# Every other pair of the stick-breaking mixer transposed in 32-blocks on VectorE, and a handicap for VectorE in the choice of engines

## The chip, the core and the metric

The kernel runs on one core of one Trainium2 chip. The metric is the device time of one execution in microseconds. Before the change the median of three runs is 1145.74 us (1144.85 to 1147.17). A separate execution was recorded by the hardware profiler; it took 1142.08 us, 1140.3 us of them between its first and its last instruction.

The engines go by the names of the profile: PE (TensorE), PEld (its weight loads), DVE (VectorE), ACT (ScalarE), POOL (GpSimd), SP (SyncE, which issues most DMAs).

## What is computed

Two layers of a decoder trunk, 512 tokens wide and 1024 features deep, all in float32. Each layer normalises its input, projects it, runs three causal token mixers side by side on the projections and merges them through gates. The mixer that the change is about is the third one, stick-breaking attention with 8 heads of 64:

```python
def hybrid_layer(x, c_silu, ...):
    u = rms_norm(x, norm_g) * (1 + scale) + shift
    z = u @ w_in        # split into aq ak av ag iq ik iw  bq bk bv bg  cq ck cv cg  ma mb mc
    ya = dsa_attention(...)            # A: indexer picks 128 keys per query, softmax attention
    yb = swa_sinks_attention(...)      # B: window of 128 keys, softmax with a sink
    yc = stick_breaking_attention(cq, ck, cv)
    merged = sum(sigmoid(m_b) * ((y_b * silu(gate_b)) @ w_br_b) for b in "abc")
    return x + gate * (merged @ w_out)

def stick_breaking_attention(q, k, v):       # per block of 128 queries
    z = einsum('bthd,bshd->bhts', qb, k) * dh ** -0.5
    log_1m = where(strict, log_sigmoid(-z), 0)
    after = reverse_cumsum(log_1m) - log_1m
    a = where(strict, exp(log_sigmoid(z) + after), 0)
    return einsum('bhts,bshd->bthd', a, v)
```

## The kernel before

All products of a projection run on PE as three passes of 512 columns: each weight chunk of 128 rows is loaded into `wstage`, split into a high part `whi` (a cast) and a low part `wlo` (a subtraction), and multiplied as `whi*uh + whi*ul + wlo*uh`. So PE's work on one chunk of four 128-row blocks is twelve matmuls of 512 columns, and ACT, DVE or POOL do one cast and one subtraction for it.

The mixers work on pairs of heads, four pairs (0 to 3) each, in the order C, B, A. For a pair of the C mixer, `c_qk(p)` (L1191) multiplies queries by keys into five PSUM banks (`ps_s`), in high parts first and then in one uninterrupted group of low parts (`low_parts`, L1179). The value product of the pair before rides in that same group (`RIDE`, L51): pair 0's in `c_qk(1)`, pair 1's in `c_qk(2)`, pair 2's in `c_qk(3)`; pair 3's comes alone afterwards (`GROUPS`). Each bank then goes through a mask, |z|, exp, ln and a reverse scan on DVE (`tensor_tensor_scan`, 511 columns), and a last exp on ACT leaves the weights in a tile `t`, queries in the partitions.

The value product needs keys in the partitions, so the weights of a pair are transposed first, in `softmax_tr`. There are two ways:

- the way of the C mixer before: 20 PE transposes of 128 x 128 (`ps_s<-small,t` in the profile; `small` holds the identity) into five banks, and five copies of 512 columns into the tile `U` on ACT or DVE (`U<-ps_s`);
- the way of the A and B mixers (`TR32`, L47): the normalising step writes the weights in a strided layout into one tile `X` (one buffer for all mixers), four DVE instructions transpose its 32 x 32 blocks in place (`STREAM_TRANSPOSE X<-X`), and sixteen DMAs, issued by SP or ACT as each quarter is ready, move blocks between partition quarters into `U` or, for odd pairs of A and B, into `V5`. In `value_run` (L1404) PE then reads the keys of such a pair in steps.

Nothing runs in the order in which it is written. A `Recorder` collects all instructions with the engines that each may run on, and `forward` (L431) lists them by their latest start, over five rounds (L290), with costs from a table. For an instruction that may run on several engines, `elsewhere` (L558) asks whether another engine would end it earlier; if so, it isn't given to this one. The casts (`cast`: ACT, DVE, and POOL unless the source is in PSUM), the subtractions (`both`: DVE or POOL) and some other steps have such a choice; PE's work has none. DMAs of the 32-block way may be issued by SP or ACT. Each engine then runs its own list strictly in order, so an instruction that waits holds back all behind it on its engine.

In each layer the C mixer runs beside the indexer's selection of keys (`score`, DVE max and match-replace), the gate projections and the queries and keys of the mixers to come. What fills PE between the mixers' steps are the merge gates' projections and the branch products. After the last value product of A comes only such filling and the output projection.

Of the kernel before, what the change touches and what calls it, by code (L numbers as in the profile page):

```python
# [25 lines left out]
F32 = mybir.dt.float32  # L26
F32R = mybir.dt.float32r
BF16 = mybir.dt.bfloat16
AF = mybir.ActivationFunctionType
# [4 lines left out]
P = 128  # L34
# [9 lines left out]
QCOST = 2408  # L44
BKEY = "cfree2"
LOAD_AHEAD, SPLIT_AHEAD = 4, 3
TR32 = {'a': (0, 1, 2, 3), 'b': (0, 1, 2, 3)}  # L47
RIDE = {('c', 1): (0,), ('c', 2): (1,), ('c', 3): (2,), ('a', 1): (0,)}
GROUPS = {'c': ((3,),), 'a': ((1, 2), (3,)), 'b': ((0, 1), (2, 3))}

# [231 lines left out]
class Recorder:  # L282
# [5 lines left out]
    ENTER = {"m": 0.0, "t": 0.035, "c": 0.17, "r": 0.17}  # L288
    TOPORT = 0.13
    ROUNDS = 5  # L290

    def __init__(self, tc, nc, psum, sbuf):
        self.tc, self.nc, self.psum, self.sbuf = tc, nc, psum, sbuf
# [263 lines left out]

    def elsewhere(self, x, name, at, E):  # L558

        end = at + x.alts[name].cost  # L560
        for o, y in x.alts.items():
            if o != name:
                t = max(E[o]["free"], x.est, x.soft.get(o, 0.0), E[o]["port"] if y.port else 0.0) + y.cost
                if t < end - 1e-9:
                    return True
        return False

# [80 lines left out]
def trunk(ctx, tc, xT, vecs, w_ss, w_gt, w_first, w_t, w_v, w_br, w_o, rope, consts, out):  # L648
# [7 lines left out]
    rec = Recorder(tc, nc, ps, sb)  # L656
# [54 lines left out]
    csb, o = small[:, 0:8], 8  # L711
# [63 lines left out]
    st = {}  # L775
# [415 lines left out]
    def c_qk(p):  # L1191
        def fn():
            q = st[f"cq{p}"]
            kh, kl = st[f"ck{p}"]
            zb, pt = [None] * 5, [None] * 5
            for i in (3, 2, 0, 1):
                ts, W = slice(128 * i, 128 * i + 128), 128 * i + 128
                o, first = [None] * 2, [False] * 2
                for e in range(2):
                    bk, c0 = apos(e, i)  # L1200
                    if zb[bk] is None:
                        zb[bk], first[e] = sbank(), True
                    o[e] = zb[bk][:, c0:c0 + W]
                for e in range(2):
                    mm(o[e], q[:, e, ts], kh[:, e, :W], first[e])
                if i == 1:
                    mm(o[1], q[:, 1, ts], kl[:, S:], False)
            low_parts(q, kl, apos, zb, "c", p, LOW_ALL)
            for bk in (0, 3, 1, 4, 2):
                z = zb[bk]  # L1210
                if bk % 3:
                    m = z[:, 256:].rearrange("p (a b) -> p a b", a=2) if bk != 2 else z.rearrange("p (a b) -> p a b", a=2)[:, :, 128:]
                    DVE.tensor_tensor(out=m, in0=m, in1=cmask.unsqueeze(1).to_broadcast([P, 2, P]), op=OP.add)
                else:
                    DVE.tensor_tensor(out=z[:, 384:], in0=z[:, 384:], in1=cmask, op=OP.add)
                t = pt[bk] = t512("t", 10)
                u32 = mybir.dt.uint32
                rec.add({"ACT": ("activation", (t, z, AF.Abs), {}),
                         "DVE": ("tensor_scalar", (t.bitcast(u32), z.bitcast(u32), 0x7FFFFFFF, None), dict(op0=OP.bitwise_and))})
                ACT.activation(t, t, AF.Exp, scale=-1.0)  # L1220
                ACT.activation(t, t, AF.Ln, bias=1.0)
                DVE.scalar_tensor_tensor(t, z, 0.0, t, op0=OP.min, op1=OP.subtract)
                fill(t[:, 511:512], BIG)
                back = t[:, 0:511][:, ::-1]
                DVE.tensor_tensor_scan(back, z[:, 1:512][:, ::-1], back, BIG, op0=OP.add, op1=OP.subtract)
                ACT.activation(t, t, AF.Exp, scale=-1.0)
            st["p", p] = pt
        return op(2700, fn)

    def mixer_c():  # L1230
# [19 lines left out]
    def apos(e, i):  # L1250
        return ((1 + 3 * e, 384), (2, 256 * e), (1 + 3 * e, 0), (3 * e, 0))[i]
# [553 lines left out]
```

## Time and profile before

| | before |
|---|---|
| median of 3 runs | 1145.74 us |
| lowest, highest | 1144.85, 1147.17 us |
| the profiled execution | 1142.08 us |
| its span | 1140.3 us |
| granted clock of PE, mean | 0.996 |
| instructions | 17580 |

The page gives the busy time of each engine, the chain of work that ended last and the groups of instructions. A group's row reads: line, engine, operation, tiles written and read, shape and count, then the busy time of the whole group, the mean duration of one in ns, and the idle time of the engine ahead of them with what ended it. Most instructions have line L620, where the recorder emits them, and those of the uninterrupted low-part and value groups L618; so groups are told apart by their tiles. In the stages, a row gives the busy time of each engine in a stretch of the span, with the number of its instructions.

### The profile page before, as it was taken

To read this page: it belongs to the slowest core of one execution; us is meant where nothing else is said; L and a number is where in the kernel's file an instruction comes from. 1 tells how busy PE (TensorE), PEld (TensorE's weight loads), DVE (VectorE), ACT (ScalarE), POOL (GpSimd) and SP (SyncE) were. 2 spreads that over 40 slices of the span, in tenths; PEclk is the share of its full clock that TensorE was granted. 3 is DMA by queue.
4 is the path that set the end of the run, shared out by engine and by line. 5 is a ranking of instruction groups with operands and counts; after the bars stand their busy time and mean duration, and the time that the engine had idled before them with its cause. 6 is when DMAs were issued, how large, how long until landed. Compare 5 with 4: busy or idle time off the path is not lost.

```text
span 1140.3 us, 17580 instructions
## 1 busy us (share of the span) xinstructions
PE 1123.2 (99%) x5619; PEld 932.7 (82%) x5619; DVE 984.5 (86%) x2238; ACT 530.2 (46%) x1125; POOL 169.4 (15%) x237
## 2 busy tenths in 40 slices
PE   8999999999999999999999999999999999999997
PEld 6899878788887778788898998877888778877886
DVE  7977999999999987888686589999999999777765
ACT  5633767563446442433143247766435455433122
POOL 0100336310013200000000004551101221000001
PEclk9999999999999999999999999999999999999999
DMA  9744332445464573545634442234645455534343
GB/s 351 236 120 122 93 93 84 111 143 152 116 173 148 161 218 121 166 140 177 195 101 108 109 138 78 81 93 121 167 120 139 140 148 147 150 84 142 99 124 107
DMA packets 92764, 157.23 MB, mean 138 GB/s; under 512 B 14080, under 2 KB 28672, under 8 KB 92672
## 3 DMA queue, kind: packets, MB, share of 16 engines
q1 hardware_dynamic: 84608, 143.98, 43.2%
q10 hardware_dynamic: 8064, 12.13, 3.7%
q8 instruction: 44, 0.72, 0.3%
q14 instruction: 48, 0.39, 0.1%
HBM read 125.39 MB, written 4.19 MB: 114 GB/s over the span
## 4 chain that ended last, share of the span: by engine, by line
PE 82%; DVE 11%; DMA 2%; issue 2%; ACT 1%; SPq 0%; POOL 0%; DVEq 0%; ACTq 0%; POOLq 0%
PE ps_z L620 64%; PE ps_s L620 15%; DVE t L620 3%; PE ps_s L618 3%; DVE m L620 1%; DVE score L620 1%; DVE wlo L620 1%; PE ps_z L618 1%; DVE X L620 1%; DMA Y<-in_w_ss 1%; DVE zc L620 1%; DVE Y L620 1%; DVE e L620 0%; SPq L620 0%; DMA V<-X 0%
## 5 line engine op out<-in xcount | busy, mean ns | idle before, releaser
L620 PE MATMUL ps_z<-uh,whi 128*128 128x512 f32 (+1 forms) x905 | 354.1, 393 | 3.7 <-DVE sm L620 2.2
L620 PE MATMUL ps_z<-ul,whi 128*128 128x512 f32 (+1 forms) x905 | 353.1, 391 | 0.3 <-DVE ul L620 0.3
L620 PE MATMUL ps_z<-uh,wlo 128*128 128x512 f32 (+1 forms) x905 | 352.0, 390 | 0.0
L620 DVE TENSOR_TENSOR wlo<-wstage,whi 128x512 fp32r<-128x512 f32 (+2 forms) x322 | 210.8, 657 | 12.4 <-ACT whi L620 4.5
L620 PEld LDWEIGHTS ps_z<-uh,whi 128*128 128x128 f32 x905 | 170.2, 188 | 38.9 <-DVE sm L620 2.6
L620 PEld LDWEIGHTS ps_z<-ul,whi 128*128 128x128 f32 x905 | 170.3, 188 | 34.4 <-issue 1.2
L620 PEld LDWEIGHTS ps_z<-uh,wlo 128*128 128x128 f32 x905 | 170.3, 188 | 34.4 <-issue 0.2
L620 DVE CAST whi<-wstage 128x512 fp32r<-128x512 f32 (+1 forms) x200 | 81.0, 406 | 89.3 <-PE ps_z L620 72.7
L620 ACT CAST whi<-wstage 128x512 fp32r<-128x512 f32 (+2 forms) x122 | 73.0, 601 | 112.6 <-PE ps_z L620 67.7
L620 PE MATMUL ps_z<-Y,whi 128*128 128x512 f32 x384 | 118.5, 389 | 0.0
L620 ACT ACTIVATE e<-ps_z 128x512 f32<-128x512 f32 x68 | 40.4, 594 | 120.6 <-PE ps_z L620 89.4
L620 ACT ACTIVATE t<-t,nm 128x256 f32<-128x256 f32 (+3 forms) x128 | 65.2, 511 | 46.4 <-DVE nm L620 21.8
L620 POOL TENSOR_TENSOR wlo<-wstage,whi 128x512 fp32r<-128x512 f32 (+2 forms) x50 | 63.8, 1277 | 138.6 <-PE ps_z L620 52.3
L620 PEld LDWEIGHTS ps_z<-Y,whi 128*128 128x128 f32 x384 | 72.1, 188 | 15.0
L620 ACT ACTIVATE e<-e 128x512 f32<-128x512 f32 x96 | 59.8, 630 | 49.6 <-DVE e L620 47.2
L620 POOL CAST whi<-wstage 128x512 fp32r<-128x512 f32 (+1 forms) x50 | 30.6, 613 | 335.3 <-PE ps_z L620 236.9
L620 PE MATMUL ps_z<-Y,wlo 128*128 128x512 f32 x192 | 74.7, 389 | 0.0
L620 ACT ACTIVATE t<-t 128x512 f32<-128x512 f32 x120 | 67.0, 629 | 0.9
L620 DVE MAX8 m<-score 128x8 f32<-128x256 f32 (+2 forms) x96 | 53.2, 554 | 1.4
L620 PE MATMUL ps_s<-KH,Q 128*128 128x256 f32 (+3 forms) x280 | 50.9, 305 | 2.1 <-ACT U L620 0.9
L620 DVE MATCH_REPLACE8 score<-m,score 128x256 f32<-128x256 f32 (+2 forms) x96 | 52.0, 542 | 0.1
L620 PEld LDWEIGHTS ps_s<-KH,Q 128*128 128x128 f32 x280 | 42.5, 189 | 9.6 <-ACT U L620 1.8
(218 smaller groups left out, 1952.0 us busy)
## 6 DMA issues: line engine op xcount, KB each, us to landing
wstage<-in_w_t SPq DMA_DIRECT2D x212, 256.0 KB, 2.7
wstage<-in_w_v SPq DMA_DIRECT2D x48, 182.0 KB, 2.4
m<-zs SPq DMA_DIRECT2D x128, 64.0 KB, 2.0
wstage<-in_w_gt SPq DMA_DIRECT2D x32, 256.0 KB, 2.7
wstage<-in_w_ss SPq DMA_DIRECT2D x32, 256.0 KB, 2.8
wstage<-in_w_o SPq DMA_DIRECT2D x32, 256.0 KB, 2.7
Y<-in_w_ss SPq DMA_DIRECT2D x15, 512.0 KB, 5.6
wstage<-in_w_first SPq DMA_DIRECT2D x16, 256.0 KB, 3.2
```

The costliest lines, as they stand in the source:

```text
L618: self.real[engine].matmul(*[real(a) for a in q[:3]], start=q[3], stop=True, skip_group_check=True)
L620: made = getattr(self.real[engine], y.op)(*[real(a) for a in y.args], **{k: real(v) for k, v in y.kw.items()})
```

## The change

Pairs 1 and 3 of the C mixer take the 32-block way in both layers. Their last exp is split by head and query block, eight ACT instructions instead of five, and writes into `X`; the transposes and DMAs are those of the A mixer. And `elsewhere` adds 0.2 us to the end of any instruction with a choice when it weighs DVE, so that work goes to ACT or POOL unless DVE would end it more than 0.2 us sooner.

```diff
-TR32 = {'a': (0, 1, 2, 3), 'b': (0, 1, 2, 3)}
+TR32 = {'a': (0, 1, 2, 3), 'b': (0, 1, 2, 3), 'c': (1, 3)}
...
     ROUNDS = 5
+    FAVOUR = 0.2
...
     def elsewhere(self, x, name, at, E):
 
-        end = at + x.alts[name].cost
+        end = at + x.alts[name].cost + (self.FAVOUR if name == "DVE" else 0.0)
         for o, y in x.alts.items():
             if o != name:
                 t = max(E[o]["free"], x.est, x.soft.get(o, 0.0), E[o]["port"] if y.port else 0.0) + y.cost
-                if t < end - 1e-9:
+                if t + (self.FAVOUR if o == "DVE" else 0.0) < end - 1e-9:
                     return True
...
-            zb, pt = [None] * 5, [None] * 5
+            zb, pt, X = [None] * 5, [None] * 5, None
...
-                ACT.activation(t, t, AF.Exp, scale=-1.0)
-            st["p", p] = pt
+                if p not in TR32.get("c", ()):
+                    ACT.activation(t, t, AF.Exp, scale=-1.0)
+                    continue
+                if X is None:
+                    X = rec.tile("X", [P, 20 * P], F32)
+                for e in range(2):
+                    for i in range(4):
+                        b_, c0 = apos(e, i)
+                        if b_ == bk:
+                            W = 128 * i + 128
+                            ACT.activation(strided(X, "c", e, i), t[:, c0:c0 + W].split((W // P, 4, 32), (0, 1, 2)), AF.Exp, scale=-1.0)
+            st["p", p] = X or pt
```

Because the recorder lists everything anew, the two edits move instructions all over the program. In number, over both layers:

| engine: instruction | before | after |
|---|---|---|
| PE: transposes `ps_s<-small,t` | 160 | 80 |
| DVE and ACT: copies `U<-ps_s`, 512 columns | 14 and 26 | 4 and 16 |
| DVE: `STREAM_TRANSPOSE X<-X`, 640 columns | 32 | 48 |
| ACT: exps and lns `t<-t` of 512; exps `X<-t` of 128 to 512 | 120; 0 | 100; 32 |
| casts `whi`, 512 wide: DVE, ACT, POOL | 156, 103, 49 | 69, 175, 64 |
| casts `whi`, 364 wide: DVE, ACT, POOL | 38, 10, 0 | 2, 38, 8 |
| subtractions `wlo`, 512 wide: DVE, POOL | 261, 47 | 234, 74 |
| DMAs issued: SP, ACT | 730, 152 | 774, 172 |

First place: PE in layer 1, where pair 2's scores are made and pair 1's value product rides along. `KH`, `Q` and `klow` are keys and queries, `U` the transposed weights, `V` the values, `uh`, `ul`, `whi`, `wlo` a projection. Before, the high parts of the scores, the low parts and the value product stand together:

```order
L620 MATMUL ps_s<-KH,Q 128x256 x2
L620 MATMUL ps_s<-klow_80,Q 128x256
L618 MATMUL ps_s<-klow_80,Q 128x512 x2
L618 MATMUL ps_s<-klow_80,Q 128x384 x2
L618 MATMUL ps_s<-klow_80,Q 128x256
L618 MATMUL ps_s<-klow_80,Q 128x128 x2
L618 MATMUL ps_z<-U,V_671 64x512 x2
```

With the change, PE leaves the scores after their high parts and goes on with a projection:

```order
L621 MATMUL ps_s<-KH,Q 128x256 x2
L621 MATMUL ps_s<-klow_80,Q 128x256
L621 MATMUL ps_z<-uh_215,whi 128x512
L621 MATMUL ps_z<-ul_253,whi 128x512
L621 MATMUL ps_z<-uh_215,wlo 128x512
L621 MATMUL ps_z<-uh_278,whi 128x512
```

In all, 33 matmuls of 512 columns now stand between the high parts and the group of low parts and value product. Between pair 0's and pair 1's value product the list holds 73 projection matmuls of 512 columns and 20 transposes before, and 105 and none now; between pair 1's and pair 2's 72 before and 55 now, with 20 transposes in both; between pair 2's and pair 3's 84 and 20 before, and 98 and none now. Layer 2 is listed alike.

Second place: DVE in layer 1, behind the scans of pair 1 (the rows of 511 columns). Before, the key selection and a split follow, and somewhat later come two copies of transposed weights:

```order
L620 TENSOR_TENSOR klow_80<-ps_z,KH 64x512
L620 MATCH_REPLACE score_1217<-m_1649,score_1217 128x256
L620 TENSOR_SCALAR mods_76<-dotg,small 128x1
L620 MAX m_1830<-score_1217 128x8
L620 TENSOR_TENSOR G<-ps_z,e 128x512
L620 MATCH_REPLACE score_1217<-m_1830,score_1217 128x256
L620 TENSOR_TENSOR wlo<-wstage,whi 128x512
L620 SCALAR_TENSOR_TENSOR wstage,dotg<-wstage,csr 128x512
L620 MAX m_1854<-score_1217 128x8
L620 COPY U<-ps_s 128x512 x2
```

With the change the four block transposes stand there:

```order
L621 TENSOR_TENSOR klow_80<-ps_z,KH 64x512 x2
L621 TENSOR_SCALAR e<-e 128x512
L621 TENSOR_TENSOR wlo<-wstage,whi 128x512
L621 STREAM_TRANSPOSE X<-X 128x640 x2
L621 TENSOR_TENSOR G<-ps_z,e 128x512
L621 MATCH_REPLACE score_1218<-m_1658,score_1218 128x256
L621 STREAM_TRANSPOSE X<-X 128x640 x2
L621 TENSOR_TENSOR wlo<-wstage,whi 128x512
```

Counted over DVE's list from the indexer's first sum to the first step of the B mixer, in each layer alike: eight block transposes, two `wlo` and two `KH` subtractions come in; five copies to `U`, six steps of 512 columns with a choice (subtractions, rotations, a scaling), one |z| and two casts go to ACT or POOL, and four steps of the key selection go to a later place on DVE.

## The prediction

> **What bounds the kernel now.** I read the first part of the page, then the busy time by stage, then PE's own waits. First the page's busy times:
>
> ```profile
> PE 1123.2 (99%) x5619; PEld 932.7 (82%) x5619; DVE 984.5 (86%) x2238; ACT 530.2 (46%) x1125; POOL 169.4 (15%) x237
> ```
>
> PE is busy 99% of the span, DVE 86%. By stage (columns: PE, PEld, DVE, ACT, POOL):
>
> ```profile
> 0.00:55.00 55.00, 50.85 (x237) 40.86 (x238) 47.57 (x96) 33.37 (x64) 4.54 (x12) 1.00 0.86 299
> 110.00:215.00 105.00, 104.54 (x543) 84.02 (x541) 103.04 (x201) 73.12 (x135) 47.27 (x74) 1.00 0.33 90
> 300.00:420.00 120.00, 115.59 (x547) 92.36 (x546) 116.03 (x293) 62.77 (x156) 19.72 (x22) 0.99 0.59 170
> 671.00:776.00 105.00, 104.57 (x543) 84.23 (x541) 103.04 (x201) 73.00 (x134) 47.16 (x74) 1.00 0.32 89
> 860.00:980.00 120.00, 119.49 (x574) 97.33 (x573) 116.07 (x278) 64.95 (x157) 24.30 (x25) 1.00 0.52 145
> 1060.00:1140.00 80.00, 73.25 (x367) 61.91 (x365) 50.16 (x97) 20.63 (x36) 3.56 (x5) 0.97 0.37 112
> ```
>
> The C mixer runs in 110 to 215 and 671 to 776. PE has half a microsecond free there and DVE two: both are full, while ACT has 32 us and POOL 58. PE's other free time is the start (4.2 us), the last stage (6.8 us) and the A mixer of layer 1 (4.4 us). What PE waited for inside the layers is short:
>
> ```profile
> PE ps_z L620 <- DVE sm L620: 2.2, 1, 2.2
> PE ps_z L620 <- DVE zc L620: 1.6, 1, 1.6
> PE ps_s L620 <- ACT U L620: 0.9, 2, 0.5
> PEld ps_s L618 <- DMA U<-X: 0.4, 1, 0.4
> ```
>
> So time follows PE's work, and DVE is close behind it exactly where the change works.
>
> **The change part by part: PE.** PE's list of matmuls in time (start, duration, count) shows a group of ten transposes between projections:
>
> ```profile
> 155.35 0.39 PE L620 MATMUL ps_z<-uh,whi 128*128 128x512 f32 x1
> 155.58 0.39 PE L620 MATMUL ps_z<-ul,whi 128*128 128x512 f32 x1
> 155.81 0.39 PE L620 MATMUL ps_z<-uh,wlo 128*128 128x512 f32 x1
> 156.04 1.25 PE L620 MATMUL ps_s<-small,t 128*128 128x128 f32 x10
> 157.04 0.48 PE L620 MATMUL ps_z<-uh,whi 128*128 128x512 f32 x1
> 157.36 0.52 PE L620 MATMUL ps_s<-small,t 128*128 128x128 f32 x3
> ```
>
> Starts of 512 columns lie 0.23 us apart; durations overlap, so I count starts. The ten transposes hold the next start back from 156.04 to 157.04, and the matmul behind them takes 0.32 instead of 0.23 to the following start: 1.00 + 0.09 = 1.09 us for ten, 0.109 each. Eighty of them go: -8.7 us. Nothing hides them, since PE has no room in these stages; at the least they could be worth nothing, if PE then waits.
>
> The Trainium skill ("Perfetto Trace Analysis", section "Identifying the Most-Contended Engine") holds that busy matmul time misjudges PE and that the weight loads' busy share is the measure. By that rule PE would have the 18% that PEld lacks, and the sum would be 0 instead of -8.7. The starts 0.23 us apart speak for the sum; the rule is a rival below.
>
> Does PE read the pairs in steps more slowly? A value product from PE-transposed weights, and one of the A mixer in steps, by the recorded time of their sixteen parts:
>
> ```profile
> 166.27 2.38 PE L618 MATMUL ps_z<-U,V 128*64 128x512 f32 x16
> 377.48 2.37 PE L618 MATMUL ps_z<-U,va 128*64 128x512 f32 x16
> ```
>
> 2.38 and 2.37: nothing.
>
> The two waits of PE for ACT's copies, 0.9 us, stand after pair 3's transposes in each layer, whose banks the B mixer's scores then take. Those copies go: -0.9 us, or 0 if the scores have then to wait for something else; I take the whole, since the order gives PE more projections there.
>
> **The new path of pairs 1 and 3.** It runs from the exp through four block transposes and sixteen DMAs to the value product. Prices of the transposes, the copies and the splits, then of issuing a DMA (min/median/max), and of its landing (the median, in the last column):
>
> ```profile
> L620 DVE STREAM_TRANSPOSE X<-X 128x640 f32<-128x640 f32 x32 | 24.5, 813 | 0.0
> L620 DVE COPY U<-ps_s 128x512 f32<-128x512 f32 x14 | 9.2, 681 | 0.1
> L620 DVE TENSOR_TENSOR wlo<-wstage,whi 128x512 fp32r<-128x512 f32 x261 | 178.2, 684 | 10.4 <-ACT whi L620 4.5 <-POOL whi L620 1.1 <-DVE whi L620 0.5
> L620 ACT CAST whi<-wstage 128x512 fp32r<-128x512 f32 x103 | 63.8, 619 | 101.3 <-PE ps_z L620 67.1 <-DMA V<-X 16.4 <-issue 5.2
> L620 DVE CAST whi<-wstage 128x512 fp32r<-128x512 f32 x156 | 65.7, 422 | 60.7 <-PE ps_z L620 53.9 <-PE ps_s L620 6.5
> L620 POOL TENSOR_TENSOR wlo<-wstage,whi 128x512 fp32r<-128x512 f32 x47 | 60.9, 1295 | 73.9 <-DVE whi L620 37.0 <-ACT whi L620 18.8 <-DVE Y L620 7.5
> L620 DVE CAST whi<-wstage 128x364 fp32r<-128x364 f32 x38 | 13.2, 348 | 27.0 <-PE ps_z L620 17.2 <-PE ps_s L620 9.7
> L620 ACT CAST whi<-wstage 128x364 fp32r<-128x364 f32 x10 | 5.0, 498 | 9.0 <-PE ps_s L620 8.4 <-ACT Q L620 0.6
> L620 ACTq DMA_DIRECT2D U<-X x74: 514/554/1562, 237.4 to 983.9; - x74
> U<-X SPq DMA_DIRECT2D x30, 80.0 KB, 2.8
> DMA to landing us min/median/max: 1.9/2.9/4.4
> ```
>
> From ready `X`: four transposes 4 x 0.77 = 3.1 us (24.5 / 32 each), the last quarter's issues about 2 x 0.55, a landing of 2.9: some 7 us. Before, it was 20 transposes of 0.109 and five copies on two engines, near 4 us. So the value product can come 3 us later. PE's new order covers it: from pair 0's to pair 1's value product, 32 more projections of 0.23 less 20 transposes of 0.109 are 5.2 us more work; for pair 3, 14 more less 20 transposes give 1.0 us, and the B mixer's high parts, now ahead of it, most of the rest. Twelve such pairs of A and B cost PE one wait of 0.4 us, so four more cost 0.1 us by that row. At the worst each has the longest issue and landing, 1.0 + 1.5 = 2.5 us over the medians, 10 us for four. The uninterrupted group stalls PE's whole queue when it waits, and pair 2's scores with it, for its low parts stand in the same group. I take 0.15 each, near the low end, because the rows of A and B are the same transfers: +0.6 us.
>
> **DVE in the C mixer.** It gains 8 x 0.77 + 4 x 0.68 = 8.9 us a layer (transposes, subtractions) and loses five copies (3.3 at 0.66), six steps of 512 columns (4.1), a |z| (0.65), two casts (0.85) and four steps of key selection (1.9), 10.8 in all: -2.0 us. The copies and the handicap pay for the transposes. Counted at nothing on the path, because it stays within the 105 us; without that relief it would be +6.1 against 2.0 free, the last rival.
>
> **ACT, POOL, SP.** ACT gets 72 + 28 casts (72 x 0.62 + 28 x 0.50 = 59 us), twenty DMA issues (11) and loses ten copies (5): about 65 us more on 530 busy and 84 of issuing (152 x 0.55), in 1140. POOL gets 27 subtractions of 1.3 and some casts, about 70 us on 169. SP gets 44 issues, 25 us. None is full, so all this counts as nothing. What queues behind: on ACT, a cast behind a DMA that waits for DVE's transpose, and PE for that cast; on SP, the weight loads behind up to nine `U<-X` issues, 5 us. The weights are prepared ahead, and in the trace ACT's casts came late for this by
>
> ```profile
> ACT whi L620 <- DMA V<-X: 16.4, 4, 5.9
> ```
>
> 16.4 us in all, without a wait of PE for `whi` in its list. With the handicap DVE also sheds work in the A and B stages: 87 casts of 0.42 over the program, 36 of 0.35, 27 subtractions of 0.68, 68 us together. That could end PE's 4.4 us of gaps in 300 to 420, where DVE is busy 116 of 120; between nothing and -4.9 (with 0.5 in layer 2). I count nothing, as the gaps' last releasers (`sm`, `zc`) are steps DVE must do in any case. The start and the last stage are lists of DVE and ACT steps with few changes: nothing, within a microsecond either way.
>
> **Sum.** -8.7 - 0.9 + 0.6 = -9.0 us. Against the profiled execution, 1142.08 becomes 1133.1. The three timed runs have a median 3.7 us above it; I carry the difference over: 1145.74 - 9.0 = 1136.7 us.
>
> **The rivals.**
>
> *More than PE's part.* The relief of DVE also closes the A mixer's gaps: -9.0 - 4.9 = -13.9, 1131.8 us. For it: DVE is at 97% there. Against: layer 2 has the same DVE load and PE waits only 0.5 us.
>
> *No change.* Either the four value products each wait 2.5 us, +10.0 against -8.7 and no other term, 1147.0 us; for it, every transfer shares SP and ACT with weight loads and casts; against it, the one wait in twelve. Or PE has room after all, and fewer matmuls only widen its gaps: 1145.7 us. Against that stand the starts without gaps; this is what the skill's rule on weight loads would give.
>
> *Slower: DVE becomes the bound of the C mixer.* The block transposes cost DVE 6.1 us a layer, and if the subtractions on POOL hold DVE up for as long as they relieve it, 6.1 - 2.0 free = 4.1 us a layer are added, and PE's saving in that stage becomes idle time: 2 x 4.1 = +8.2, 1153.9 us. It decides as soon as DVE's net in the stage passes +2 us, 4 us from where the order puts it. For it: 103.04 of 105. Against: POOL's list from the first to the last of its one-column fills, that is in that stage, adds up to no more than before. The Trainium skill ("VectorE: DVE Perf Modes", section "Rules for kernel authors") advises PE for a transpose of 128 x 128 and leaves VectorE the 32 x 32 blocks. The trace agrees on the bare prices: 0.109 us on PE against 0.15 on DVE for 128 columns, DMAs apart. By that rule the change spends 16 x 0.77 = 12.3 us of DVE to save 8.7 on PE, 3.6 us lost wherever DVE binds.
>
> That the change does nothing can't be: 80 transposes are gone from PE's list.
>
> **How the numbers follow.** About 0.2% (2.3 us) is what a measurement of this kernel can tell from no change. The forecast has 0.58, more than PE's part 0.14: faster 0.72. No change has 0.15 (late transfers 0.10, room on PE 0.05), slower 0.13. The range runs from the first rival, less a microsecond for the start, 1131, to late transfers at their worst, 1147; it leaves out the slower case.
>
> **What would show it.** Right: PE's transposes at 80, the C stages shorter or holding more projections at the same PE share, PE's idle time still near 17 us, waits for `U<-X` under 1 us, DVE's busy time down by 70 us or more. Wrong: gaps on PE ahead of the low parts of pair 2 or pair 3's value product with `U<-X` as releaser; PE waiting for `whi` from ACT or `wlo` from POOL; DVE full in the C stages with PE idle.

## The result, and the profile after

The changed kernel takes 1134.64 us in the median of four runs (1133.6 to 1134.9). The kernel before, in the same session, takes 1145.3 us (four runs, 1143.06 to 1147.17). The ratio is 0.9906, with a 95% interval of 0.9887 to 0.9925: 10.7 us less. The forecast of 9.0 us less lies inside that interval. The profiled execution took 1133.6 us, 1131.7 of them its span; the forecast for it was 1133.1.

The first line of the page after (busy time, share of the span, instructions):

```profile
PE 1113.8 (98%) x5539; PEld 922.8 (82%) x5539; DVE 921.6 (81%) x2016; ACT 607.0 (54%) x1285; POOL 237.5 (21%) x307
```

PE has 80 instructions fewer and is busy for 9.4 us less (not all of it because of the transposes, as the kernel with the handicap alone will show); its idle time, span less busy time, is 17.9 us against 17.1. DVE's busy time is down by 63 us, ACT's up by 77, POOL's by 68.

The stages of after, in the columns of the prediction:

```profile
0.00:55.00 55.00, 51.71 (x239) 41.42 (x240) 45.47 (x90) 36.00 (x70) 8.82 (x15) 1.00 0.84 299
110.00:215.00 105.00, 104.06 (x524) 83.03 (x522) 103.33 (x196) 72.91 (x140) 46.23 (x73) 1.00 0.38 107
300.00:420.00 120.00, 116.63 (x556) 93.75 (x555) 112.99 (x275) 67.39 (x157) 29.09 (x31) 1.00 0.59 170
671.00:776.00 105.00, 103.86 (x525) 82.02 (x525) 103.31 (x207) 70.98 (x135) 48.88 (x75) 1.00 0.42 118
860.00:980.00 120.00, 118.93 (x569) 96.47 (x568) 105.18 (x241) 66.33 (x155) 29.16 (x31) 1.00 0.53 152
```

In the C mixer (110 to 215, 671 to 776) DVE is as full as before, at 103.3 of 105, and PE is 0.5 and 0.7 us less busy. PE gets more projections done there: the stretch from 110 to 215 holds 342 projection matmuls of 512 columns before and 356 now, the one from 671 to 776 342 and 345. In the stage with the A mixer of layer 1 (300 to 420) DVE is down from 116 to 113.

What PE and its weight loads waited for in after (total, times, longest):

```profile
PE ps_s L621 <- DVE t L621: 3.2, 6, 1.0
PE ps_z L619 <- DMA m<-zs: 2.5, 1, 2.5
PE ps_s L619 <- DMA U<-X: 0.2, 1, 0.2
```

```profile
PEld ps_s L619 <- DMA U<-X: 0.6, 1, 0.6
```

The two waits for ACT's copies (0.9 us) are gone. The waits that name `U<-X` are as short as forecast; the two rows are one stall of pair 3 in layer 2, of PE and of its weight loads. Pair 3 in layer 1 has one more, of 0.5 us: the last transfer of its `U` lands at 218.64 and the product starts at 219.10. New are three more short waits for `t` (six instead of three, 3.2 us instead of 1.8), the DVE steps that read the score banks of the C mixer, and one of 2.5 us, ended at 373.3, ahead of a value product of A in layer 1. That wait is put down to `m<-zs`, which the product doesn't read; the transfers of its own `U` were issued until 371.3, as ACT's list in time shows (start, duration):

```profile
362.81 8.54 ACTq L621 DMA_DIRECT2D U<-X  x9
371.39 1.26 ACT L621 CAST Q<-zc 64x512 fp32r<-64x512 f32 x2 [9.73 <-DMA U<-X]
```

Nine issues hold ACT for 8.5 us there, and a cast waits behind them. The last of these transfers lands at 373.01, 2.3 us after its issue began, and PE starts 0.3 us later: it is this transfer that PE waited for, and it belongs to the A mixer, not to the new pairs.

So the total is right. Whether it is made of the right parts can't be read from these two traces, because the two edits always came together.

### The profile page after: what moved, and what is told of

Read it like the earlier page. It is cut to its first block, busy times and chain, and to the rows that moved or that the text cites. A ratio compares the mean times of both kernels' runs of the same rounds, so it can differ in the third digit from the quotient of the medians.

```text
span 1131.7 us, 17615 instructions
## 1 busy us (share of the span) xinstructions
PE 1113.8 (98%) x5539; PEld 922.8 (82%) x5539; DVE 921.6 (81%) x2016; ACT 607.0 (54%) x1285; POOL 237.5 (21%) x307
## 4 chain that ended last, share of the span: by engine, by line
PE 77%; DVE 15%; DMA 4%; SPq 1%; ACT 1%; issue 1%; POOL 0%; DVEq 0%; ACTq 0%; POOLq 0%
PE ps_z L621 60%; PE ps_s L621 14%; DVE t L621 4%; PE ps_s L619 2%; DVE X L621 1%; SPq L621 1%; DVE wlo L621 1%; DMA m<-zs 1%; PE ps_z L619 1%; DVE score L621 1%; DVE m L621 1%; DMA U<-X 1%; DVE zc L621 1%; DVE e L621 1%; DMA Y<-in_w_ss 1%
## 5 line engine op out<-in xcount | busy, mean ns | idle before, releaser
L621 DVE TENSOR_TENSOR wlo<-wstage,whi 128x512 fp32r<-128x512 f32 (+2 forms) x294 | 193.2, 661 | 99.2 <-ACT whi L621 90.0
L621 ACT CAST whi<-wstage 128x512 fp32r<-128x512 f32 (+2 forms) x226 | 133.7, 593 | 234.2 <-PE ps_z L621 176.2
L621 POOL TENSOR_TENSOR wlo<-wstage,whi 128x512 fp32r<-128x512 f32 (+2 forms) x78 | 99.7, 1279 | 230.5 <-DVE whi L621 116.5
L621 POOL CAST whi<-wstage 128x512 fp32r<-128x512 f32 (+1 forms) x72 | 43.6, 606 | 318.4 <-PE ps_z L621 177.6
L621 ACT ACTIVATE t<-t 128x512 f32<-128x512 f32 x100 | 56.1, 627 | 0.3
L621 DVE STREAM_TRANSPOSE X<-X 128x640 f32<-128x640 f32 (+1 forms) x80 | 55.9, 738 | 0.4 <-ACT X L621 0.2
L621 ACT ACTIVATE e<-ps_z 128x512 f32<-128x512 f32 x68 | 40.3, 593 | 22.1 <-DVE wlo L621 5.2
```

Source lines behind the costliest of these rows:

```text
L621: made = getattr(self.real[engine], y.op)(*[real(a) for a in y.args], **{k: real(v) for k, v in y.kw.items()})
```

## The theories

- **PE's work** (the prediction's): time follows PE's list. 80 transposes less are 8.7 us; the handicap only pays for what DVE gets.
- **Relief of DVE**: from the indexer to the A mixer DVE is a second bound that PE's busy time hides. The handicap is worth time by itself, and the pairs without it cost time.
- **Transfers**: the sixteen DMAs of each new pair cost time somewhere, whatever DVE does.
- **Chance of the list**: any edit makes a new list, and this alone moves the time by some microseconds either way.

All fourteen kernels in numbers. "PE idle" is the span less PE's busy time in the profiled execution; ratios are those of the timed runs to the kernel before.

| kernel | PE instructions | PE busy | PE idle | DVE busy | ratio (95%) |
|---|---|---|---|---|---|
| before | 5619 | 1123.2 | 17.1 | 984.5 | 1 |
| the change | 5539 | 1113.8 | 17.9 | 921.6 | 0.9906 (0.9887 to 0.9925) |
| pairs only | 5539 | 1119.4 | 32.9 | 992.2 | 1.0093 (1.0080 to 1.0107) |
| handicap only | 5619 | 1119.3 | 15.2 | 918.4 | 0.9948 (0.9935 to 0.9960) |
| all four pairs | 5459 | 1117.2 | 45.4 | 942.9 | 1.0188 (1.0170 to 1.0206) |
| change, idle PE transposes | 5619 | 1121.1 | 25.2 | 923.9 | 1.0047 (1.0029 to 1.0065) |
| before, idle DVE blocks | 5619 | 1125.9 | 27.4 | 994.7 | 1.0117 (1.0098 to 1.0135) |
| before, idle DMAs | 5619 | 1126.3 | 24.7 | 987.5 | 1.0074 (1.0056 to 1.0091) |
| handicap, idle DVE blocks | 5619 | 1118.5 | 14.1 | 924.8 | 0.9924 (0.9906 to 0.9943) |
| handicap, idle DMAs | 5619 | 1125.4 | 22.1 | 921.7 | 1.0020 (1.0009 to 1.0031) |
| change, handicap 0.1 | 5539 | 1120.1 | 34.4 | 983.1 | 1.0088 (1.0069 to 1.0108) |
| change, handicap 0.25 | 5539 | 1114.0 | 20.4 | 909.1 | 0.9924 (0.9910 to 0.9939) |
| change, handicap 0.4 | 5539 | 1117.8 | 26.1 | 890.6 | 0.9994 (0.9984 to 1.0005) |
| change, pair 3 only | 5579 | 1117.5 | 23.1 | 919.1 | 1.0026 (1.0012 to 1.0039) |

Below, a ratio is turned into microseconds with the 1144 us of the kernel before in those sessions.

Four pairs of kernels differ by the handicap alone: before and handicap only, pairs only and the change, idle blocks without and with it, idle DMAs without and with it. In each the handicap of 0.2 gains: 6, 21, 22 and 6 us. Chance of the list alone would hardly give one sign four times.

## The experiments: one edit without the other

**The pairs without the handicap.**

```diff
-    FAVOUR = 0.2
+    FAVOUR = 0.0
```

> The pairs alone, the handicap set to 0: 80 PE transposes as in the change, but DVE keeps its casts (215 whi casts on DVE against 74 with the change and 200 before). Theory 'PE's work' (the gain is the 80 transposes that PE no longer issues, 8.7 us; the handicap only makes room for them): 8 to 10 us faster than before, 1136 to 1137. Rival 'relief of DVE' (the gain is the handicap's, the transposes only change places): within 2 us of before. Rival 'room' (without the handicap the block transposes overload DVE in the C stages): PE's saving is kept only in part, 3 to 6 us faster, with more waits of PE for DVE than in the change.

None of the three theories had told this: it is slower than the kernel before, 1155.17 us, 10.7 us more, where the change is 10.7 us less. The first line of its page, and its longest waits of PE:

```profile
PE 1119.4 (97%) x5539; PEld 925.5 (80%) x5539; DVE 992.2 (86%) x2258; ACT 527.2 (46%) x1134; POOL 158.8 (14%) x216
```

```profile
PE ps_z L621 <- DVE zc L621: 5.6, 3, 3.3
PE ps_z L621 <- DVE G L621: 4.2, 3, 2.0
```

PE has as many instructions as in the change, and 15 us more idle time. Its longest waits are for DVE's steps: `zc` (queries and keys of the mixers to come) and `G` (gates, whose reading frees a PSUM bank). PE's saving has become idle time and more. By stage, the two C mixers lie in the first and third of these rows, the A mixers, with the end of B, in the others:

```profile
110.00:215.00 105.00, 101.36 (x509) 80.94 (x508) 102.13 (x188) 72.88 (x139) 39.00 (x61) 1.00 0.35 101
300.00:420.00 120.00, 111.39 (x522) 88.03 (x521) 115.36 (x292) 61.97 (x155) 29.99 (x29) 0.99 0.53 154
671.00:776.00 105.00, 101.48 (x511) 81.30 (x510) 101.49 (x193) 71.92 (x138) 35.91 (x58) 1.00 0.36 101
860.00:980.00 120.00, 116.59 (x555) 93.76 (x554) 115.73 (x300) 61.64 (x155) 24.51 (x25) 0.99 0.49 137
```

Against the rows of before in the prediction, PE loses 6.3 us more in the two C stages and 7.1 us more in the two A stages.

**The handicap without the pairs.**

```diff
-TR32 = {'a': (0, 1, 2, 3), 'b': (0, 1, 2, 3), 'c': (1, 3)}
+TR32 = {'a': (0, 1, 2, 3), 'b': (0, 1, 2, 3)}
```

> The handicap alone: all 160 PE transposes stay, DVE sheds 114 of its 200 whi casts. Theory 'PE's work': PE's work is that of before, so within 2 us of before, at best the 4.9 us of gaps in the A mixer's stages. Rival 'relief of DVE': 8 us or more faster than before.

1137.43 us: 6 us less than before, with all 160 transposes on PE. That is less than "relief of DVE" had told (8 or more) and near the most that "PE's work" allowed (4.9): with an interval of 4.6 to 7.4 us, this run alone doesn't part the two.

```profile
PE 1119.3 (99%) x5619; PEld 931.2 (82%) x5619; DVE 918.4 (81%) x2018; ACT 606.2 (53%) x1279; POOL 236.1 (21%) x303
```

So more than half of what the change brings is there without the pairs. The 4.8 us between this kernel and the change (1 to 8 by the ends of the two intervals) are what the pairs add, about half of their 8.7 us. The gain isn't all a gain of waits: of the 5.8 us between the profiled executions of before and of this kernel, PE's idle time accounts for 1.9 (17.1 and 15.2). PE is also busy for 3.9 us less with the same number of instructions: 1.7 of these are the slow stretch behind a gap of PE at 415.9 in before (last section), which this kernel doesn't have, and the rest isn't explained.

How full DVE is shows in the stretch from the indexer's first sum to the last step of the key selection (`score<-score`, the ends of whose rows give the last start in layer 2). The steps of DVE that write `score`, for before, the change, the pairs only and the handicap only (min/median/max, first and last start):

```profile
L620 DVE TENSOR_SCALAR score<-score x6: 293/340/417, 191.7 to 909.9; 128x256 f32<-128x256 f32 x2, 128x384 f32<-128x384 f32 x2, 128x512 f32<-128x512 f32 x2
```

```profile
L621 DVE TENSOR_SCALAR score<-score x6: 282/344/1131, 238.6 to 877.8; 128x256 f32<-128x256 f32 x2, 128x384 f32<-128x384 f32 x2, 128x512 f32<-128x512 f32 x2
```

```profile
L621 DVE TENSOR_SCALAR score<-score x6: 277/352/503, 260.5 to 927.7; 128x256 f32<-128x256 f32 x2, 128x384 f32<-128x384 f32 x2, 128x512 f32<-128x512 f32 x2
```

```profile
L621 DVE TENSOR_SCALAR score<-score x6: 274/346/421, 188.5 to 857.4; 128x256 f32<-128x256 f32 x2, 128x384 f32<-128x384 f32 x2, 128x512 f32<-128x512 f32 x2
```

And the stages from the indexer to about that end in layer 2, for before and for the pairs only (columns PE, PEld, DVE, ACT, POOL):

```profile
667.00:909.00 242.00, 241.06 (x1217) 195.63 (x1216) 237.51 (x554) 137.03 (x294) 63.91 (x92) 1.00 0.42 118
```

```profile
667.00:927.00 260.00, 254.01 (x1260) 205.97 (x1259) 251.00 (x590) 142.84 (x313) 62.06 (x86) 1.00 0.44 126
```

In before DVE is busy for 237.5 of 242 us, so the selection ends when DVE's list is through: at 909.9. With the pairs alone it ends 18 us later, with the handicap alone 52 us earlier, in the change 32 us earlier (all from the span's start, so with what layer 1 brings). The A mixer's first step that reads `score` shows when this matters; in layer 2, for before and for the handicap only:

```profile
L620 DVE CUSTOM_DVE_ANT_0 t<-ps_s,score x24: 394/551/692, 911.2 to 1019.0; 128x384 f32<-128x384 f32 x8, 128x512 f32<-128x512 f32 x8, 128x256 f32<-128x256 f32 x8
L621 DVE CUSTOM_DVE_ANT_0 t<-ps_s,score x24: 405/548/692, 901.1 to 1013.2; 128x384 f32<-128x384 f32 x8, 128x512 f32<-128x512 f32 x8, 128x256 f32<-128x256 f32 x8
```

In before it starts 1.3 us later than the selection's last step: the selection has no time to spare. With the handicap it starts 44 us later than that step, so the selection no longer sets the time of the A mixer. In before PE is just as full there and hides it. In the pairs-only kernel PE loses 6.0 us in this stretch instead of 0.9, with DVE busy for 251 of 260.

**All four pairs, with the handicap of 0.2.**

```diff
-TR32 = {'a': (0, 1, 2, 3), 'b': (0, 1, 2, 3), 'c': (1, 3)}
+TR32 = {'a': (0, 1, 2, 3), 'b': (0, 1, 2, 3), 'c': (0, 1, 2, 3)}
```

> All four pairs of the C mixer by 32-blocks, with the handicap: no PE transpose of weights is left, 96 block transposes. Theory 'PE's work': another 8.7 us less work on PE than the change; but DVE's list of the C stage adds up to 123.6 us by the rows of before where the stage of before had 118.7 for 105 us of time, that is 109 us at the same overlap, 4 us more than the stage is long now. So the gain stops where DVE binds: 1126 (all of it) to 1134 (none beyond the change). Rival 'relief of DVE': slower than the change by DVE's 6.1 us a layer, 1140 or more.

1164.62 us, 21 us slower than before, although PE has 160 instructions fewer: as the rival had told (1140 or more), and far from "PE's work". Its page, and the first of PE's waits:

```profile
PE 1117.2 (96%) x5459; PEld 921.0 (79%) x5459; DVE 942.9 (81%) x2041; ACT 592.4 (51%) x1267; POOL 235.5 (20%) x308
```

```profile
PE ps_s L621 <- DVE t L621: 15.9, 18, 1.7
```

PE is idle for 45 us, and its granted clock is 0.988 in the mean, against 0.996 before. Here the new bound is in the C mixer itself, in both layers: 18 waits for `t`, 15.9 us. That is the place that the prediction's slower rival named.

## The experiments: one cost alone

**The change, with the 80 PE transposes done for nothing.** In each of the two pairs PE transposes the identity 20 times into score banks that nobody reads.

```diff
+            if b == "c":
+                for k in range(5):
+                    tb = sbank()
+                    for j in range(4):
+                        PE.transpose(tb[:, 128 * j:128 * j + 128], ident, ident)
```

> The change, with 20 PE transposes of the identity for each pair 1 and 3 of the C mixer, into banks that nobody reads: PE has its 80 transposes back without copies, and ACT and DVE do what they do in the change. Theory 'PE's work': slower than the change by 80 x 0.109 = 8.7 us, 1143 to 1144. Rival 'relief of DVE': within 2 us of the change.

1147.94 us, 13.3 us over the change for 8.7 us of PE work, 4 us more than forecast. PE's busy time rises by 7.3 us and its idle time by 7.3. The work is really on the path, as the prediction had it; the other waits come with a new list (the idle transposes also take score banks), and this run can't divide them up.

**Before, with the block transposes for nothing**, into an `X` that nobody reads, for pairs 1 and 3; without and with the handicap:

```diff
+            if b == "c" and p % 2:
+                X = rec.tile("X", [P, 20 * P], F32)
+                for k in range(5):
+                    DVE.transpose(X[:, 512 * k:512 * k + 512], pt[k])
```

> Before, with five DVE block transposes of 512 columns from the finished weights of pairs 1 and 3 into a tile that nobody reads, 6 us of DVE a layer, no DMA, and all PE transposes kept. Theory 'DVE binds' (from the indexer to the end of the key selection DVE is busy but for 4.4 of 247 us, so what is put on it there delays the A mixer, and PE's list stands still for it): 8 to 20 us slower than before, 1152 to 1164, with the end of the key selection 6 us or more later. Rival 'transfers' (the pairs alone lost time through their sixteen DMAs and what waits behind them): within 3 us of before. Rival 'chance of the list' (each new list of the planner falls some us this or that way): within 4 us either way.

> The handicap alone (1137.4) with the same idle block transposes. Theory 'DVE binds': the handicap has made room, the key selection ended 51 us earlier with it than before, so the 6 us a layer cost less than in the kernel before, 2 to 6 us: 1139 to 1143. If DVE did not bind, 1137 within 2 us; if the handicap's gain had another cause than room on DVE, as much as in the kernel before, 8 us or more.

On the kernel before the blocks cost 13.4 us (1157.72 us), as "DVE binds" had told, and the key selection of layer 2 ends 15 us later, at 925.3. On the handicap-only kernel they cost nothing, where 2 to 6 us were expected: 1134.76 us, a ratio of 0.9924 (0.9906 to 0.9943) beside 0.9948 (0.9935 to 0.9960). The selection ends 19 us later there, at 876.7, and the A mixer's first step still comes 24 us after it. The pages of the two:

```profile
PE 1125.9 (98%) x5619; PEld 933.4 (81%) x5619; DVE 994.7 (86%) x2266; ACT 526.8 (46%) x1118; POOL 170.2 (15%) x236
```

```profile
PE 1118.5 (99%) x5619; PEld 931.3 (82%) x5619; DVE 924.8 (82%) x2026; ACT 607.8 (54%) x1279; POOL 246.1 (22%) x315
```

PE's list has the same length in both; its idle time is 27.4 us in the one and 14.1 in the other. This tells "PE's work" from "relief of DVE" most clearly: the same addition on DVE is dear where the handicap is missing and free where it is there. Where it is dear, on the kernel before, the loss is not in the C mixer:

```profile
110.00:215.00 105.00, 104.93 (x541) 84.28 (x540) 103.19 (x196) 71.52 (x132) 44.18 (x70) 1.00 0.31 89
860.00:980.00 120.00, 113.78 (x537) 91.26 (x536) 113.89 (x290) 60.86 (x155) 25.14 (x26) 0.99 0.49 135
```

PE is full in the C stage and loses 6.2 us in the A stage of layer 2, where before had 0.5. So the 6.3 us that the pairs alone lose in the C stages don't come from DVE's busy time by itself. In that kernel PE waits there for `G`, for ACT's `t`, and ahead of pair 1's value product (1.3 and 1.0 us); how these divide between the new path's transfers and the new list isn't shown.

**Before, with sixteen DMAs for nothing** in each of the two pairs; without and with the handicap:

```diff
+            if b == "c" and p % 2:
+                X = rec.tile("X", [P, 20 * P], F32)
+                for b_ in range(4):
+                    for a_ in range(4):
+                        how = ("dma_start", (X[32 * b_:32 * b_ + 32, 512 * a_:512 * a_ + 512], pt[b_][32 * a_:32 * a_ + 32, :]), {})
+                        rec.add({"SP": how, "ACT": how})
```

> Before, with sixteen DMAs of 64 KB from the finished weights of pairs 1 and 3 into a tile that nobody reads, issued by SP or ACT, and nothing more on DVE. Theory 'DVE binds': within 3 us of before. Rival 'transfers': 8 us or more slower than before. Rival 'chance of the list': within 4 us either way.

> The handicap without the pairs (0.9948 by itself), and sixteen DMAs of 64 KB a pair, issued by SP or ACT, into a tile that nobody reads, for pairs 1 and 3. On the kernel before the same DMAs cost 8 us (1.0074). Transfers (they cost what they cost, whatever VectorE does: queues and memory): about 8 us again, ratio near 1.002. Relief of DVE (the DMAs cost only because they hold up steps of a VectorE that has no room, and with the handicap it has): no more than 2 us, ratio 0.993 to 0.997. Chance of the list: any value within 3 us of the handicap alone, which this run can't tell from the second.

They cost 8.5 us on the kernel before (1152.44 us) and 8.2 us on the handicap-only kernel (1.0020 against 0.9948). So "transfers" had it right in both runs, and relief of DVE, which had told that the second would be nearly free, is wrong for the DMAs: they cost the same with DVE full and with DVE relieved. The 8 us are not lost where the DMAs stand. With the handicap, the C mixer of layer 1 and the first large gap of PE behind it read:

```profile
110.00:215.00 105.00, 104.40 (x539) 82.92 (x539) 102.14 (x201) 73.27 (x136) 48.56 (x77) 1.00 0.39 109
342.00:348.00 6.00, 3.72 (x27) 2.48 (x24) 3.38 (x7) 1.54 (x3) 1.46 (x2) 1.00 0.52 154
```

PE is nearly full in the C mixer and loses 2.3 us in one piece at 345.4, between the B mixer's last value products and the A mixer's first scores. SP, DVE and PE at that gap, from their lists in time (start, duration; in brackets the idle time before and what ended it):

```profile
330.34 7.85 SPq L621 DMA_DIRECT2D V<-X  x10
...
339.39 2.41 SPq L621 DMA_DIRECT2D m<-zs  x4
```

```profile
344.98 0.69 DVE L621 TENSOR_TENSOR m<-m,rt 128x512 f32<-128x512 f32 x1 [2.58 <-DMA m<-zs]
345.71 0.69 DVE L621 TENSOR_TENSOR zc<-zc,m 128x512 f32<-128x512 f32 x1
...
346.93 1.28 DVE L621 TENSOR_TENSOR e<-ps_s,G 128x512 f32<-128x512 f32 x2
```

```profile
347.67 0.44 PE L621 MATMUL ps_s<-KH,Q 128*128 128x384 f32 x1 [2.28 <-DVE e L621]
```

Ten transfers of B hold SP for 7.85 us; the four `m<-zs` that rotate a query come behind them, and DVE waits 2.6 us for those. Behind them on DVE stands `e`, which reads a score bank, and PE's next scores start when that is read, at 347.67. So what bites here are SP's and DVE's lists in order. This gap is 2.3 of the 6.9 us by which PE is longer idle than with the handicap alone. Whether the idle DMAs cost this through SP's list, through the tiles `t` and `X` that they hold longer, or only by making another list, the runs don't settle.

## The experiments: the size of the handicap, and one pair

**A handicap of 0.1, 0.25 and 0.4 with the pairs.**

```diff
-    FAVOUR = 0.2
+    FAVOUR = 0.1
```

and likewise with 0.25 and 0.4.

> The change with a handicap of 0.1 us in place of 0.2. With 0 it is 1.0093, with 0.2 it is 0.9906. Relief of DVE (the casts and subtractions go over by degrees): in between, 0.995 to 1.003, with VectorE's busy time between 992 and 922 us. PE's work alone: 0.992, as with 0.2, for PE's work is the same. Chance of the list: anywhere from 0.988 to 1.01, without order.

> The change with a handicap of 0.25 us in place of 0.2: a near neighbour, to see how much a new listing alone moves the time. Relief of DVE: nearly the same balance, a part of the way to what 0.4 gives (0.9994), so 0.990 to 0.994. Chance of the list: 3 to 5 us away from the change, either way, at a VectorE busy time that is nearly the same; then the last 3 us of any difference here are not explained by mechanisms.

> The change with a handicap of 0.4 us: DVE gives away all its whi casts, POOL's list grows from 243 to 316 us. Theory 'DVE binds': PE's waits of 5.9 us over the handicap alone shrink, 2 to 6 us faster than the change, 1129 to 1133. Rival 'POOL takes DVE's place' (its subtractions take 1.28 us against 0.66, and hold DVE up on shared inputs): slower than the change, 1137 or more.

In order of the handicap, 0, 0.1, 0.2, 0.25, 0.4: ratios 1.0093, 1.0088, 0.9906, 0.9924, 0.9994, with DVE busy for 992, 983, 922, 909 and 891 us. So 0.1 is no middle, though relief of DVE had expected one (0.995 to 1.003): it takes hardly any work off DVE and gains nothing. The group rows tell why that can be. In the kernel with 0.1 the casts that DVE kept, and in the change those that ACT got:

```profile
L621 DVE CAST whi<-wstage 128x512 fp32r<-128x512 f32 (+2 forms) x178 | 72.6, 409 | 92.3 <-PE ps_z L621 73.3
```

```profile
L621 ACT CAST whi<-wstage 128x512 fp32r<-128x512 f32 (+2 forms) x226 | 133.7, 593 | 234.2 <-PE ps_z L621 176.2
```

A cast takes 0.41 us on DVE and 0.59 on ACT, shapes mixed; by shape in the prediction's rows it is 0.42 and 0.62 for 512 columns, 0.35 and 0.50 for 364. Where both are free, a handicap under the difference leaves the cast on DVE, and one above gives it to ACT. The planner's own price table (`price` in the kernel) has this difference: by its formulas, with the overlap that it grants each engine, ACT is dearer by 0.19 us at 512 columns and by 0.15 at 364, so 0.2 passes both and 0.1 neither.

The neighbour 0.25 isn't told from 0.2 (its interval overlaps), as relief of DVE had told. At 0.4 the gain is gone: 1143.55 us, where "DVE binds" had 1129 to 1133 and its rival, POOL in DVE's place, 1137 or more. There PE waits as follows:

```profile
PE ps_z L621 <- DVE G L621: 4.8, 2, 2.5
PE ps_s L621 <- DVE t L621: 3.7, 5, 1.2
PE ps_s L619 <- DMA wstage<-in_w_t: 1.9, 1, 1.9
```

DVE has the least work of all and is still late with `G` and `t`: less work on an engine is not the same as having its steps in time. DVE waits for ACT's casts in this kernel for 102.5 us over 82 times, against 90.0 in the change, and for POOL's for 24.4 against 6.4; that this makes `G` late is argued, not shown.

**The change for pair 3 alone.**

```diff
-TR32 = {'a': (0, 1, 2, 3), 'b': (0, 1, 2, 3), 'c': (1, 3)}
+TR32 = {'a': (0, 1, 2, 3), 'b': (0, 1, 2, 3), 'c': (3,)}
```

> The change for pair 3 alone, with the handicap of 0.2. PE has 40 transposes less than with the handicap alone, 4.4 us. PE's work: 0.9948 less 0.0038, so 0.991. Relief of DVE (VectorE has room for one pair without giving any of PE's saving back): the same 0.991 or, as its pair asks for half of the transposes of the change, at least as good as the change. Dose: the change's pairs brought 4.8 us over the handicap alone, so half of them 2.4: 0.9927. Chance of the list: within 3 us of these.

A miss for all of them, chance included, which had 3 us to either side: 1147.21 us (1142.41 to 1151.87), slower than before, and 9 us slower than the handicap with no pair at all. PE's longest wait, and PE in layer 2 at that place:

```profile
PE ps_s L619 <- DMA U<-X: 7.4, 2, 3.8
```

```profile
778.65 0.39 PE L621 MATMUL ps_z<-Y,wlo 128*128 128x512 f32 x1
782.61 1.73 PE L619 MATMUL ps_s<-U,V 128*64 128x512 f32 x8 [3.57 <-DMA U<-X]
```

Pair 3's value product waits 3.8 us in layer 1 and 3.6 in layer 2 for its transposed weights. SP's own waits between 210 and 225 us tell what its last `U<-X` issues waited for:

```profile
SPq L621 <- DMA wstage<-in_w_t: 3.3, 1, 3.3
```

By this row SP stood for 3.3 us behind the landing of a weight load before it issued the last four `U<-X` (at 219.95). The row may not name the cause: ACT too issued none of its `U<-X` between 216.3 and 218.9, and transfers of the same pair issued at 213.3 to 214.6 took 5.5 to 5.8 us to land, where the median in before is 2.9. This is the late transfer that the prediction priced at 2.5 us at worst, and it is longer. The profiled execution, at 1142.41, was the fastest of twelve, so some 5 us of this kernel's median are not in its trace.

## Why the prediction was right, and which step failed

**PE's term was right in kind, and somewhat large.** Time does follow the transposes: put back as idle work, they cost 13.3 us. By the busy time of PE they are worth 5.5 us (from the handicap alone to the change), 7.3 (put back as idle work) or, from before to the change, 9.4 less the slow stretch of 1.7 that only before has, 7.7; the prediction had 8.7. No room on PE appeared, so the rival by weight loads is out: PEld is 82% busy in both kernels, and yet PE's list sets the time.

**The signs that the prediction named** came as told but for one: 80 transposes, more projections in the C stages, PE's idle time near 17 us (17.9), waits for `U<-X` under 1 us, the waits for ACT's copies gone. DVE's busy time fell by 63 us, not by 70 or more.

**The step that failed is the handicap's relief: "With the handicap DVE also sheds work ... I count nothing".** The handicap alone brings 6 us. The prediction saw the possible gain (up to 4.9 us, its first rival) and put it aside because the last releasers `sm` and `zc` were steps that DVE must do in any case. That argument is wrong: a step that must be done is still late when the list ahead of it is long. With the handicap alone the wait of 2.2 us for `sm` is gone, one of 2.1 for ACT's `KH` is new, and of the 1.6 us for `zc` this is left:

```profile
PE ps_z L621 <- DVE zc L621: 1.0, 1, 1.0
```

The row of 103.04 of 105 was in the prediction; what was not read was that DVE stays at that share until the key selection ends, 242 us after the indexer's first sum, and that the A mixer begins there. The other half of that term, "DVE in the C mixer ... counted at nothing on the path", nearly held in the change: PE is idle for 2.1 us in the two C stages, 0.9 before.

**The new path is longer than its price.** The prediction had 7 us from ready weights to the value product. For pair 1 in layer 1 of the change, DVE, SP and PE read:

```profile
159.81 1.56 DVE L621 STREAM_TRANSPOSE X<-X 128x640 f32<-128x640 f32 x2
...
162.41 1.56 DVE L621 STREAM_TRANSPOSE X<-X 128x640 f32<-128x640 f32 x2
```

```profile
160.72 6.78 SPq L621 DMA_DIRECT2D U<-X  x9
```

```profile
170.63 1.08 PE L619 MATMUL ps_z<-U,V 128*64 128x512 f32 x4
```

From the first transpose to the product are 10.8 us: 4.2 for four transposes with other steps between them, 3.5 more until the last issue, and 3.1 until PE starts. The last transfer lands at 170.30, 0.3 us ahead of the product, so the list has little left over for more delay. In the change it just fits: PE waits 0.2 and 0.5 us for pair 3's transfers, against +0.6 forecast for all four. With pair 3 alone and with the handicap of 0.1 it doesn't (7.4 and 6.6 us). So +0.6 is right for this list and is no property of the change. The prediction also counted twelve pairs of A and B that go this way in the kernel before; they are sixteen (128 DMAs into `U` and 128 into `V5`), which leaves its 0.1 us as it was.

**That the sum came out is in part luck: terms that were left out or too large have opposite signs.** Handicap alone: -6.0. PE's work: -8.7. Together -14.7; measured -10.7. So the pairs bring some 4 us less than the price of their transposes: in part because that price is too large, by 1 to 3 us, in part by new waits (PE's idle time is 2.7 us longer than with the handicap alone). The first rival, with -13.9, had the better list of gains, and the forecast the better number.

**The slower rival was right for one half of the change, in part.** The pairs alone are 10.7 us slower than before (forecast +8.2 to its condition). It put the loss into the C mixer, where the pairs-only trace has 6.3 us of it; another 7.1 are in the A stages. That DVE's extra work is dear without the handicap is shown by the idle blocks (13.4 us), but they leave the C mixer full and cost in the A stages, and the idle DMAs cost 8.5 us by themselves: so DVE isn't the only cause of the loss. The handicap takes DVE's part away: not DVE's net of some 2 us in the C stage decides, as the prediction had it, but the 66 us of DVE's work that go to ACT and POOL over the program (984.5 to 918.4 with the handicap alone).

**What stays open.** What a new list by itself is worth. The handicap with idle blocks, with more work, isn't slower than without; one pair is 9 us worse than none, and idle DMAs cost 8 us for a reason that isn't shown. Of the handicap's own 6 us, some 2 have no explanation. No version here beats the change; the nearest are the handicap of 0.25 and the handicap-only kernel with idle blocks, both at 0.9924.

## What to carry to other kernels

When an edit has two parts, price each as if the other weren't there: here one alone costs 10.7 us and the other alone gains 6. Here an engine at 98% beside a full PE was a bound too, and its backlog came due at the next step that needed it, not in the stage in which it arose. A gain that depends on a re-made list holds for that list: move one step or one pair, and a covered transfer can be late.

## What the runs showed of the hardware

A gap of PE often costs more than its length. In the handicap kernel with idle DMAs, the stretch right behind the gap at 345.4 (the clock is the third figure from the end):

```profile
348.00:354.00 6.00, 6.00 (x25) 4.69 (x24) 5.44 (x16) 2.79 (x6) 3.40 (x3) 0.72 0.49 131
```

And in the kernel before, behind a gap of 2.2 us at 415.9:

```profile
418.00:424.00 6.00, 5.94 (x19) 4.73 (x20) 5.21 (x13) 1.00 (x2) 0.00 (x0) 0.72 0.82 219
```

A granted clock of 0.72 over 6 us is 6 x 0.28 = 1.7 us lost. Of the 22 gaps of PE of 2.0 us or more inside the fourteen profiles (from 60 to 1085 us), 11 were followed by such a dip and 11 were not, with no clear border: one of 2.14 us had it, one of 3.57 hadn't. Eleven more dips stand behind shorter gaps; in before with idle blocks, a gap of 1.8 us at 974.8 was enough:

```profile
977.00:983.00 6.00, 6.00 (x22) 4.82 (x21) 4.76 (x12) 4.53 (x13) 0.00 (x0) 0.72 0.54 150
```

The kernel before has one dip of this kind and the change none. The Trainium skill ("TensorE: Matmul & The Clock Gate", section "Part 1: The HAM clock gate") lets the clock fall after an idle window of about 3.4 us; here 8 of the 16 gaps between 2 and 3 us were followed by a fall already, so the runs don't bear that border out.
